# 2x2 average pooling on one core: blocks of a tile dealt out over sixteen, and engine bodies of two tiles with three result buffers

## The chip, the core and the metric

One core of a Trainium2 chip runs the kernel. Four of its instruction streams matter here: SyncE (SP), which issues the loads; VectorE (DVE), which adds; ScalarE (ACT), which scales and issues the stores; and the core's sixteen DMA engines, which move the bytes of both. The metric is the device time of one execution in microseconds (us). Before the change it is 3104.1 us, the median of nine runs that lie between 3103.82 and 3105.5.

## The reference

The input x is float32 of shape 32 x 128 x 256 x 256, kernel size and stride are 2. Each output value is the mean of a 2 x 2 window:

```python
for i in range(h_out):
    for j in range(w_out):
        window = x[:, :, i*2:i*2+2, j*2:j*2+2]
        output[:, :, i, j] = np.mean(window, axis=(2, 3))
```

The output is float32 of shape 32 x 128 x 128 x 128. So 1073.74 MB are read once and 268.44 MB are written once.

## The kernel before

The kernel views x as 524,288 rows of 512 floats: a row is the two input lines that make one output line of 128 floats. A tile is 128 partitions of 32 such rows (`TILE = 32`), that is 64 KB for each partition, 8.39 MB in all; its result is 16 KB for each partition, 2.10 MB. There are 128 tiles. `whole` is 127 of them; the last one is cut into parts of 16, 8, 4 and 4 rows a partition (`parts`), so that the end of the kernel is short.

In DRAM a tile is 128 blocks of 64 KB, one after another, and block p goes to partition p. The view `xt` says so: "(t p g) f -> t p g f". The view `ot` does the same for the result, and `block` for the parts of the last tile.

Everything stands in a critical section in which the engines' order is written out by hand, with semaphores. `take(engine, sem, n)` (line 68) waits for n and takes n off again.

- SP issues `tile_load(t, b)` (line 82, the DMA on L83) into one of two input buffers. Tiles 0 and 1 are loaded at once; every later one waits for `free[b]` first. The last tile's four parts are issued on L130, the store of tile 126 on L132. Then SP waits for the last stores: `tail`, and three of the four `stored` semaphores.
- DVE runs `tile_sum` (line 85). It waits for `loaded[b]`, adds the two input lines in place (L88), waits for the result buffer's last store (`stored[o]`, not for the first four tiles) and for its own first addition (`ready`), and adds even and odd columns into the result buffer (L92). The first four tiles are written out, then a loop has four tiles in its body, then three more are written out. The last tile's parts are on L145 and L147.
- ACT runs `tile_scale` and `tile_store` (lines 94 and 99). It waits for `summed`, gives `free[b]` to SP, multiplies by 0.25 in place (L97), waits for that, and issues the store on its own queue (L101). Again four tiles are written out, four are in the loop's body, and the rest follows. The last tile's parts are on L164 and L166.

There are four result buffers (`OUTS = 4`), taken in turn. All DMA engines serve both queues, SP's and ACT's.

Of the kernel before, what the change touches and what calls it, by code (L numbers as in the profile page):

```python
# [9 lines left out]
@with_exitstack  # L10
def kernel(
    ctx: ExitStack,
    tc: tile.TileContext,
    x: bass.AP,
    kernel_size: bass.AP,
    stride: bass.AP,
    out: bass.AP,
):
    nc = tc.nc
    P = nc.NUM_PARTITIONS  # L20

    n, c, h, w = x.shape
    k = int(kernel_size)
    s = int(stride)
    h_out = (h - k) // s + 1
    w_out = (w - k) // s + 1
    R = n * c * h_out
    units = R // P if R % P == 0 else 0


    if k == 2 and s == 2 and h % 2 == 0 and w == 256 and units >= 1024:
        _pool_2x2(ctx, tc, x, out, units)
    else:
        _generic_pool(ctx, tc, x, out, k, s, n, c, h, w, h_out, w_out)


TILE = 32
OUTS = 4


def _pool_2x2(ctx, tc, x, out, units):
    nc = tc.nc
    P = nc.NUM_PARTITIONS
    f32 = mybir.dt.float32
    w = x.shape[3]
    w_out = w // 2
    sp, act, dve = nc.sync, nc.scalar, nc.vector

    xv = x.rearrange("n c (ho a) w -> (n c ho) (a w)", a=2)
    ov = out.rearrange("n c ho wo -> (n c ho) wo")  # L50

    in_pool = ctx.enter_context(tc.tile_pool(name="inp", bufs=2))
    out_pool = ctx.enter_context(tc.tile_pool(name="outp", bufs=OUTS))
    ins = [in_pool.tile([P, TILE, 2 * w], f32, name="in_tile") for _ in range(2)]
    res = [out_pool.tile([P, TILE, w_out], f32, name="res") for _ in range(OUTS)]

    loaded = [ctx.enter_context(nc.semaphore(f"loaded{b}")) for b in range(2)]
    free = [ctx.enter_context(nc.semaphore(f"free{b}")) for b in range(2)]
    summed = ctx.enter_context(nc.semaphore("summed"))
    scaled = ctx.enter_context(nc.semaphore("scaled"))  # L60
    stored = [ctx.enter_context(nc.semaphore(f"stored{b}")) for b in range(OUTS)]
    tail = ctx.enter_context(nc.semaphore("tail"))
    ready = ctx.enter_context(nc.semaphore("ready"))
    held = ctx.enter_context(nc.semaphore("held"))

    def take(engine, sem, n=1):
        engine.wait_ge(sem, n)
        engine.sem_inc(sem, -n)  # L70

    def block(r0, g):
        rows = slice(r0, r0 + g * P)
        return xv[rows].rearrange("(p g) f -> p g f", p=P), ov[rows].rearrange("(p g) f -> p g f", p=P)

    whole, rest = divmod(units - 1, TILE)
    rest += 1
    xt = xv[0:whole * TILE * P].rearrange("(t p g) f -> t p g f", p=P, g=TILE)
    ot = ov[0:whole * TILE * P].rearrange("(t p g) f -> t p g f", p=P, g=TILE)
    loops, left = divmod(whole - OUTS, OUTS)  # L80

    def tile_load(t, b):
        sp.dma_start(out=ins[b], in_=xt[t]).then_inc(loaded[b], 16)  # L83

    def tile_sum(b, o, first=False):
        it, dst = ins[b], res[o]
        take(dve, loaded[b], 16)
        dve.tensor_add(out=it[:, :, 0:w], in0=it[:, :, 0:w], in1=it[:, :, w:]).then_inc(ready)  # L88
        if not first:
            take(dve, stored[o], 16)  # L90
        take(dve, ready)
        dve.tensor_add(out=dst, in0=it[:, :, 0:w:2], in1=it[:, :, 1:w:2]).then_inc(summed)  # L92

    def tile_scale(b, o, done):
        take(act, summed)
        act.sem_inc(free[b])
        act.mul(out=res[o], in_=res[o], mul=0.25).then_inc(done)  # L97

    def tile_store(t, o):
        take(act, scaled)  # L100
        act.dma_start(out=ot[t], in_=res[o]).then_inc(stored[o], 16)  # L101

    parts, a = [], 0
    while a < rest:
        b = rest if rest - a <= 4 else a + (rest - a) // 2
        parts.append((a, b))
        a = b

    psem = [ctx.enter_context(nc.semaphore(f"part{k}")) for k in range(len(parts))]

    with tc.tile_critical():

        for b in range(2):
            tile_load(b, b)
        with sp.Fori(2, 2 + 2 * ((whole - 2) // 2), 2) as i:
            for b in range(2):
                take(sp, free[b])
                tile_load(i + b, b)
        t = 2 + 2 * ((whole - 2) // 2)
        while t < whole:  # L120
            take(sp, free[t % 2])
            tile_load(t, t % 2)
            t += 1

        take(sp, free[whole % 2])
        it, dst = ins[whole % 2], res[whole % OUTS]
        for (a, b), s in zip(parts, psem):
            sp.dma_start(out=it[:, a:b], in_=block((whole * TILE + a) * P, b - a)[0]).then_inc(s, 16)  # L130
        take(sp, held)
        sp.dma_start(out=ot[whole - 1], in_=res[(whole - 1) % OUTS]).then_inc(stored[(whole - 1) % OUTS], 16)  # L132


        for o in range(OUTS):
            tile_sum(o % 2, o, first=True)
        with dve.Fori(0, loops) as i:
            for o in range(OUTS):
                tile_sum(o % 2, o)
        for o in range(left):  # L140
            tile_sum(o % 2, o)
        take(dve, stored[whole % OUTS], 16)
        for (a, b), s in zip(parts, psem):
            take(dve, s, 16)
            dve.tensor_add(out=it[:, a:b, 0:w], in0=it[:, a:b, 0:w], in1=it[:, a:b, w:]).then_inc(ready)  # L145
            take(dve, ready)
            dve.tensor_add(out=dst[:, a:b], in0=it[:, a:b, 0:w:2], in1=it[:, a:b, 1:w:2]).then_inc(summed)  # L147


        for t in range(OUTS):  # L150
            tile_scale(t % 2, t, scaled)
            tile_store(t, t)
        with act.Fori(OUTS, OUTS + loops * OUTS, OUTS) as i:
            for o in range(OUTS):
                tile_scale(o % 2, o, scaled)
                tile_store(i + o, o)
        for t in range(OUTS + loops * OUTS, whole):
            tile_scale(t % 2, t % OUTS, scaled if t < whole - 1 else held)
            if t < whole - 1:
                tile_store(t, t % OUTS)  # L160
        act.sem_inc(free[(whole + 1) % 2], -1)
        for a, b in parts:
            take(act, summed)
            act.mul(out=dst[:, a:b], in_=dst[:, a:b], mul=0.25).then_inc(scaled)  # L164
            take(act, scaled)
            act.dma_start(out=block((whole * TILE + a) * P, b - a)[1], in_=dst[:, a:b]).then_inc(tail, 16)  # L166


        take(sp, tail, 16 * len(parts))
        for o in range(OUTS):  # L170
            if o != whole % OUTS:
                take(sp, stored[o], 16)


def _generic_pool(ctx, tc, x, out, k, s, n, c, h, w, h_out, w_out):
# [92 lines left out]
```

## Time and profile before

| what | value |
|---|---|
| median of nine runs | 3104.1 us |
| the profiled execution's own time | 3104.78 us |
| its span in the profile | 3103.0 us |
| L88, first addition, 128x8192 | 127 times 8692 ns |
| L92, second addition, 128x4096 | 127 times 4425 ns |
| L97, scaling, 128x4096 | 127 times 3616 ns |
| load of a tile, median from issue to landing | 34.6 us |
| store of a tile, median from issue to landing | 33.9 us |
| DMA packets | 37730, 1342.21 MB |

The span is what the profiler saw between the first and the last event; the execution's own time has some more around it. In the profile, a line such as "8.69 DVE L88" in the timeline has the start, the duration, the engine and the source line of an instruction, and in brackets how long the engine was idle before it and what released it. "DVEq" is VectorE's own instruction stream, in which the waits of L70 (in `take`) stand. "SPq ... DMA_DIRECT2D" is the issue of a DMA. The DMA row of the 40 slices gives the busy share of the sixteen DMA engines in tenths. A packet is one contiguous run that one DMA engine moves: 64 KB for a load of a whole tile, 16 KB for a store of one, and 4 bytes for the write to a semaphore that each engine makes when its share has been moved.

### The profile page before, as it was taken

The page shows a single profiled execution, that of the slowest core. Times are in us where ns is not written, and L with a number is a line of the kernel's source. Part 1 is how long each engine was busy: PE and PEld are TensorE (multiplying, and loading weights), DVE is VectorE, ACT ScalarE, POOL GpSimd, SP SyncE. Part 2 cuts the span into 40 slices and gives each one's busy share as a digit, 9 for nine tenths or more (in the row PEclk, how much of TensorE's full clock was granted, in tenths as well). Part 3 has the DMA queues.
Part 4 walks back from the last instruction along what each step waited for, and adds up shares of the span by engine and source line. Part 5 has one row for each costly group of instructions (what it writes and reads, how often), then busy time and mean ns, then how long its engine had stood idle before and what let it go on. Part 6 is the DMA issues. An engine that isn't in the chain of part 4 may idle for free. (4 is left out here: it accounts for less than half of the span.)

```text
span 3103.0 us, 2444 instructions
## 1 busy us (share of the span) xinstructions
DVE 1679.7 (54%) x262; ACT 464.8 (15%) x132; POOL 0.2 (0%) x4
## 2 busy tenths in 40 slices
DVE  4555555555555555555555555555555555555555
ACT  1111111111111111111111111111111111111111
POOL 0000000000000000000000000000000000000000
DMA  9999999999999999999999999999999999999999
GB/s 415 436 439 426 436 439 425 436 440 425 437 439 425 437 439 425 437 430 434 438 439 424 441 436 424 438 439 426 436 439 424 438 440 423 438 439 423 438 438 401
DMA packets 37730, 1342.21 MB, mean 433 GB/s; under 512 B 4192, under 2 KB 4192, under 8 KB 4576
## 3 DMA queue, kind: packets, MB, share of 16 engines
q1 hardware_dynamic: 19008, 1075.85, 80.1%
q10 hardware_dynamic: 18720, 266.35, 20.1%
q14 instruction: 2, 0.02, 0.0%
HBM read 1073.74 MB, written 268.44 MB: 433 GB/s over the span
## 5 line engine op out<-in xcount | busy, mean ns | idle before, releaser
L88 DVE TENSOR_TENSOR in_tile<-in_tile 128x8192 f32<-128x8192 f32 x127 | 1103.9, 8692 | 1395.9 <-DVEq L70 1395.9
L97 ACT ACTIVATE res<-res 128x4096 f32<-128x4096 f32 x127 | 459.2, 3616 | 2587.1 <-ACTq L70 2587.1
L92 DVE TENSOR_TENSOR res<-in_tile 128x4096 f32<-128x4096 f32 x127 | 562.0, 4425 | 18.6
L145 DVE TENSOR_TENSOR in_tile<-in_tile 128x1024 f32<-128x1024 f32 (+2 forms) x4 | 9.1, 2286 | 1.3 <-DVEq L70 1.3
L97 ACT ACT_TABLE_LOAD x1 | 1.3, 1283 | 36.5 <-ACTq L70 36.5
L164 ACT ACTIVATE res<-res 128x512 f32<-128x512 f32 (+2 forms) x4 | 4.2, 1057 | 8.4 <-ACTq L70 8.4
L147 DVE TENSOR_TENSOR res<-in_tile 128x512 f32<-128x512 f32 (+2 forms) x4 | 4.9, 1225 | 0.6
L249 POOL MEMSET const-bfloat16-1.0<- 128x1 bf16 x1 | 0.1, 102 | 0.0
L249 POOL MEMSET const-uint8-127<- 128x1 uint8 x1 | 0.1, 102 | 0.0
L249 POOL MEMSET const-float32-0.0<- 128x1 f32 x1 | 0.1, 99 | 0.2 <-issue 0.2
L249 POOL MEMSET const-float32-1.0<- 128x1 f32 x1 | 0.1, 99 | 0.0
## 6 DMA issues: line engine op xcount, KB each, us to landing
out_dram<-res ACTq DMA_DIRECT2D x126, 2048.0 KB, 33.9
in_tile<-in_x_dram SPq DMA_DIRECT2D x1, 4096.0 KB, 25.1
in_tile<-in_x_dram SPq DMA_DIRECT2D x1, 2048.0 KB, 30.2
in_tile<-in_x_dram SPq DMA_DIRECT2D x2, 1024.0 KB, 33.2
out_dram<-res SPq DMA_DIRECT2D x1, 2048.0 KB, 13.8
in_tile<-in_x_dram SPq DMA_DIRECT2D x127, 34.6
out_dram<-res ACTq DMA_DIRECT2D x1, 1024.0 KB, 7.6
out_dram<-res ACTq DMA_DIRECT2D x1, 512.0 KB, 5.5
```

The lines of the kernel that those rows point to most:

```text
L88: dve.tensor_add(out=it[:, :, 0:w], in0=it[:, :, 0:w], in1=it[:, :, w:]).then_inc(ready)
L92: dve.tensor_add(out=dst, in0=it[:, :, 0:w:2], in1=it[:, :, 1:w:2]).then_inc(summed)
L97: act.mul(out=res[o], in_=res[o], mul=0.25).then_inc(done)
L145: dve.tensor_add(out=it[:, a:b, 0:w], in0=it[:, a:b, 0:w], in1=it[:, a:b, w:]).then_inc(ready)
L147: dve.tensor_add(out=dst[:, a:b], in0=it[:, a:b, 0:w:2], in1=it[:, a:b, 1:w:2]).then_inc(summed)
L164: act.mul(out=dst[:, a:b], in_=dst[:, a:b], mul=0.25).then_inc(scaled)
L249: nc = _bacc.Bacc("TRN2", target_bir_lowering=False, num_devices=1)
```

## The change

Two things are done at once.

The order by hand is written anew. There are two result buffers, taken in turn as the input buffers are, and a third one for the last tile. VectorE's loop has two tiles in its body and covers the first tiles as well; to this end each `stored[b]` is raised by 16 once before it. The wait for the result buffer's store stands ahead of the first addition now, together with the wait for the load. ScalarE's loop has two tiles in its body, with one tile written out ahead of it. The stores of tiles 125 and 126 and of the last tile's parts all raise one semaphore, `tail`, and SP waits for that alone.

The blocks of a tile are dealt out. Partition 8e + j held block 8e + j of its tile; now it holds block 16j + e, for e from 0 to 15 and j from 0 to 7. The DRAM side of each DMA has the shape 16 x 8 x run, with e outermost; the side on the chip stays 128 partitions, in their order, with one run each (`chip`). The results go back to where they belong by the same view, so the output is the same. The operations on VectorE and ScalarE keep their shapes.

```diff
-xt = xv[0:whole * TILE * P].rearrange("(t p g) f -> t p g f", p=P, g=TILE)
-ot = ov[0:whole * TILE * P].rearrange("(t p g) f -> t p g f", p=P, g=TILE)
+split = "(t j e g) f -> t e j (g f)"
+xt = xv[0:whole * TILE * P].rearrange(split, j=8, e=16, g=TILE)
+ot = ov[0:whole * TILE * P].rearrange(split, j=8, e=16, g=TILE)
...
+    def chip(tile):
+        return tile.rearrange("p g f -> p (g f)")
...
     def block(r0, g):
         rows = slice(r0, r0 + g * P)
-        return xv[rows].rearrange("(p g) f -> p g f", p=P), ov[rows].rearrange("(p g) f -> p g f", p=P)
+        split = "(j e g) f -> e j (g f)"
+        return xv[rows].rearrange(split, e=16, g=g), ov[rows].rearrange(split, e=16, g=g)
...
-    def tile_load(t, b):
-        sp.dma_start(out=ins[b], in_=xt[t]).then_inc(loaded[b], 16)
+    def load(t, b):
+        sp.dma_start(out=chip(ins[b]), in_=xt[t]).then_inc(loaded[b], 16)
...
-    out_pool = ctx.enter_context(tc.tile_pool(name="outp", bufs=OUTS))
+    out_pool = ctx.enter_context(tc.tile_pool(name="outp", bufs=3))
...
+    def sums(it, dst):
+        dve.tensor_add(out=it[:, :, 0:w], in0=it[:, :, 0:w], in1=it[:, :, w:]).then_inc(halfway)
+        take(dve, halfway)
+        dve.tensor_add(out=dst, in0=it[:, :, 0:w:2], in1=it[:, :, 1:w:2]).then_inc(summed)
+
+    def tile_sums(b):
+        take(dve, stored[b], 16)
+        take(dve, loaded[b], 16)
+        sums(ins[b], res[b])
+
+    def scale(dst, done=scaled):
+        act.mul(out=dst, in_=dst, mul=0.25).then_inc(done)
+
+    def scale_store(t, b, landed):
+        take(act, summed)
+        act.sem_inc(free[b])
+        scale(res[b])
+        take(act, scaled)
+        act.dma_start(out=ot[t], in_=chip(res[b])).then_inc(landed, 16)
...
+        for b in range(2):
+            dve.sem_inc(stored[b], 16)
+        with dve.Fori(0, whole // 2):
+            for b in range(2):
+                tile_sums(b)
+        if whole % 2:
+            tile_sums(0)
+        for a, b, part in parts:
+            take(dve, part, 16)
+            sums(it[:, a:b], dst[:, a:b])
...
+        scale_store(0, 0, stored[0])
+        pairs = (whole - 3) // 2
+        with act.Fori(1, 1 + 2 * pairs, 2) as i:
+            for b in (1, 0):
+                scale_store(i + 1 - b, b, stored[b])
+        for t in range(1 + 2 * pairs, whole - 1):
+            scale_store(t, t % 2, stored[t % 2] if t < whole - 2 else tail)
...
-        take(sp, tail, 16 * len(parts))
-        for o in range(OUTS):
-            if o != whole % OUTS:
-                take(sp, stored[o], 16)
+        take(sp, tail, 16 * (len(parts) + 2))
```

In the changed kernel the two additions stand on lines 94 and 96, the scaling on 104, the loads on 91 and 131, the stores on 111, 133 and 161.

More of the change, by code (lines that the diff above doesn't have):

```diff
@@ L37 @@
 TILE = 32
-OUTS = 4
 def _pool_2x2(ctx, tc, x, out, units):
@@ L52, in _pool_2x2, with sem @@
     in_pool = ctx.enter_context(tc.tile_pool(name="inp", bufs=2))
-    out_pool = ctx.enter_context(tc.tile_pool(name="outp", bufs=OUTS))
+    out_pool = ctx.enter_context(tc.tile_pool(name="outp", bufs=3))
     ins = [in_pool.tile([P, TILE, 2 * w], f32, name="in_tile") for _ in range(2)]
[L55 to L64, printed above, removed]
+    res = [out_pool.tile([P, TILE, w_out], f32, name="res") for _ in range(3)]
+    def sem(name):
+        return ctx.enter_context(nc.semaphore(name))
+    loaded, free, stored = [[sem(f"{n}{b}") for b in range(2)] for n in ("loaded", "free", "stored")]
+    halfway, summed, scaled, held, tail = [sem(n) for n in ("halfway", "summed", "scaled", "held", "tail")]
     def take(engine, sem, n=1):
@@ L73, in block @@
         rows = slice(r0, r0 + g * P)
-        return xv[rows].rearrange("(p g) f -> p g f", p=P), ov[rows].rearrange("(p g) f -> p g f", p=P)
+        split = "(j e g) f -> e j (g f)"
+        return xv[rows].rearrange(split, e=16, g=g), ov[rows].rearrange(split, e=16, g=g)
+    def chip(tile):
+        return tile.rearrange("p g f -> p (g f)")
     whole, rest = divmod(units - 1, TILE)
     rest += 1
-    xt = xv[0:whole * TILE * P].rearrange("(t p g) f -> t p g f", p=P, g=TILE)
-    ot = ov[0:whole * TILE * P].rearrange("(t p g) f -> t p g f", p=P, g=TILE)
-    loops, left = divmod(whole - OUTS, OUTS)
-    def tile_load(t, b):
[L83 to L101, printed above, removed]
+    split = "(t j e g) f -> t e j (g f)"
+    xt = xv[0:whole * TILE * P].rearrange(split, j=8, e=16, g=TILE)
+    ot = ov[0:whole * TILE * P].rearrange(split, j=8, e=16, g=TILE)
     parts, a = [], 0
@@ L105, in _pool_2x2 @@
         b = rest if rest - a <= 4 else a + (rest - a) // 2
-        parts.append((a, b))
+        parts.append((a, b, sem(f"part{len(parts)}")))
         a = b
-    psem = [ctx.enter_context(nc.semaphore(f"part{k}")) for k in range(len(parts))]
+    def load(t, b):
[4 more added lines that the diff above has]
+        dve.tensor_add(out=dst, in0=it[:, :, 0:w:2], in1=it[:, :, 1:w:2]).then_inc(summed)
@@ L111, in _pool_2x2 @@
+    def tile_sums(b):
[10 more added lines that the diff above has]
+        act.dma_start(out=ot[t], in_=chip(res[b])).then_inc(landed, 16)
     with tc.tile_critical():
-        for b in range(2):
-            tile_load(b, b)
@@ L115, in _pool_2x2 @@
-        with sp.Fori(2, 2 + 2 * ((whole - 2) // 2), 2) as i:
+        load(0, 0)
+        load(1, 1)
+        pairs = (whole - 2) // 2
+        with sp.Fori(2, 2 + 2 * pairs, 2) as i:
             for b in range(2):
                 take(sp, free[b])
-                tile_load(i + b, b)
-        t = 2 + 2 * ((whole - 2) // 2)
-        while t < whole:
+                load(i + b, b)
+        for t in range(2 + 2 * pairs, whole):
             take(sp, free[t % 2])
-            tile_load(t, t % 2)
-            t += 1
+            load(t, t % 2)
@@ L127, in _pool_2x2 @@
         take(sp, free[whole % 2])
-        it, dst = ins[whole % 2], res[whole % OUTS]
-        for (a, b), s in zip(parts, psem):
-            sp.dma_start(out=it[:, a:b], in_=block((whole * TILE + a) * P, b - a)[0]).then_inc(s, 16)
+        it, dst = ins[whole % 2], res[2]
+        for a, b, part in parts:
+            sp.dma_start(out=chip(it[:, a:b]), in_=block((whole * TILE + a) * P, b - a)[0]).then_inc(part, 16)
         take(sp, held)
-        sp.dma_start(out=ot[whole - 1], in_=res[(whole - 1) % OUTS]).then_inc(stored[(whole - 1) % OUTS], 16)
@@ L135, in _pool_2x2 @@
-        for o in range(OUTS):
[L136 to L147, printed above, removed]
@@ L150, in _pool_2x2 @@
[L150 to L161, printed above, removed]
@@ L162, in _pool_2x2 @@
-        for a, b in parts:
+        sp.dma_start(out=ot[whole - 1], in_=chip(res[(whole - 1) % 2])).then_inc(tail, 16)
+        for b in range(2):
[5 more added lines that the diff above has]
+            tile_sums(0)
+        for a, b, part in parts:
+            take(dve, part, 16)
+            sums(it[:, a:b], dst[:, a:b])
+        scale_store(0, 0, stored[0])
+        pairs = (whole - 3) // 2
@@ L163, in _pool_2x2 @@
+        with act.Fori(1, 1 + 2 * pairs, 2) as i:
[3 more added lines that the diff above has]
+            scale_store(t, t % 2, stored[t % 2] if t < whole - 2 else tail)
+        take(act, summed)
+        scale(res[(whole - 1) % 2], held)
+        for a, b, _ in parts:
             take(act, summed)
-            act.mul(out=dst[:, a:b], in_=dst[:, a:b], mul=0.25).then_inc(scaled)
+            scale(dst[:, a:b])
@@ L165, in _pool_2x2 @@
             take(act, scaled)
-            act.dma_start(out=block((whole * TILE + a) * P, b - a)[1], in_=dst[:, a:b]).then_inc(tail, 16)
-        take(sp, tail, 16 * len(parts))
-        for o in range(OUTS):
-            if o != whole % OUTS:
-                take(sp, stored[o], 16)
+            act.dma_start(out=block((whole * TILE + a) * P, b - a)[1], in_=chip(dst[:, a:b])).then_inc(tail, 16)
+        take(sp, tail, 16 * (len(parts) + 2))
 def _generic_pool(ctx, tc, x, out, k, s, n, c, h, w, h_out, w_out):
```

## The prediction

> **What bounds the kernel now.** I read the busy totals, then the 40 slices and the DMA queues, then the timeline of the middle and of both ends, and last the trace's records of single DMA packets.
>
> ```profile
> span 3103.0 us, 2444 instructions
> DVE 1679.7 (54%) x262; ACT 464.8 (15%) x132; POOL 0.2 (0%) x4
> ...
> DMA  9999999999999999999999999999999999999999
> ...
> q1 hardware_dynamic: 19008, 1075.85, 80.1%
> q10 hardware_dynamic: 18720, 266.35, 20.1%
> ...
> HBM read 1073.74 MB, written 268.44 MB: 433 GB/s over the span
> ```
>
> No compute engine is near full. The two queues (q1 SP: the loads, q10 ACT: the stores) together fill 100.2% of sixteen engines' span: the sixteen DMA engines are the bound, from end to end.
>
> ```profile
> 1495.34 8.69 DVE L88 TENSOR_TENSOR in_tile<-in_tile 128x8192 f32<-128x8192 f32 x1 [10.92 <-DVEq L70]
> 1504.17 4.43 DVE L92 TENSOR_TENSOR res<-in_tile 128x4096 f32<-128x4096 f32 x1
> 1508.80 3.62 ACT L97 ACTIVATE res<-res 128x4096 f32<-128x4096 f32 x1 [20.57 <-ACTq L70]
> 1508.95 48.70 SPq L83 DMA_DIRECT2D in_tile<-in_x_dram  x3
> 1512.65 0.34 ACTq L101 DMA_DIRECT2D out_dram<-res  x1
> 1519.51 8.69 DVE L88 TENSOR_TENSOR in_tile<-in_tile 128x8192 f32<-128x8192 f32 x1 [10.91 <-DVEq L70]
> ```
>
> Here one sees a tile's period: 1519.51 - 1495.34 = 24.17 us (24.19 between 3042.93 and 3067.10 at the end). VectorE stands idle 10.9 us of it and ScalarE 20.6. A load is issued at 1508.95, 13.6 us after the sums began, with the next tile's load still under way for 10.6 us. So SP has about 9 us in hand before the engines could run dry (1.3 us goes from an issue to the first packet: issued 0.96, first packet at 2.2).
>
> The packet records carry the point. An engine moves eight 64 KB packets of a load and eight 16 KB packets of a store per tile. A 64 KB packet lasts 2.418 us in the median, at the 1st percentile, and 2.420 at the 99th; a 16 KB packet 0.611 at all three. 8 x (2.418 + 0.611) = 24.2 us: the period, with nothing left. The slope, 49152 bytes in 1.807 us, is 27.2 GB/s an engine, 435 for sixteen. And the engines keep step: from the third load on, first and last of the sixteen complete 2.255 or 2.256 us apart, every time.
>
> ```profile
> 3093.98 1.22 DVE L145 TENSOR_TENSOR in_tile<-in_tile 128x1024 f32<-128x1024 f32 x1
> ...
> 3096.89 0.34 ACTq L166 DMA_DIRECT2D out_dram<-res  x1
> ```
>
> The ends are short: nothing moves for the first 2.2 us, and 9.0 us lie between the last load part's first sum and the end, of which the last store needs most. All that order, waits and buffers could give back is below 2.2 + 9.0 minus the stores that still run there: 3103.0 - 128 x 24.19 = 6.7 us, 0.2%.
>
> [...]
>
> **The change, part by part.**
>
> *Dealt-out blocks (`block`, `xt`, `ot`, `chip`).* Bytes, packets and packet sizes stay: the contiguous run is still one block of 64 KB or 16 KB. The DRAM side is now [16, 8, run] against 128 partitions. [...]
> [...] A tile's load is eight such rounds: 38.7 us. [...] Period 38.7 against 24.19: +14.5 us x 128 = +1856 us. Bounds of this unknown: nothing, [...] to 48.5 - 24.2 = 24.3 us a tile[...] (8 x 2 x 3.029 = 48.5). I take 38.7 because engines that start within 0.75 us of one another and then keep step for 127 tiles have no visible reason to drift apart by half a load[...].
> [...]
>
> *Two result buffers in place of four.* `tile_sums` now waits for the store of two tiles back before the first addition. A store is issued 17.3 us after its tile's sums began (1512.65 - 1495.34) and lands 33.9 us after that (the page's median): 51.2, and the sums of the tile two on begin at 48.4. VectorE would wait some 2.8 us, and behind it the two sums, the scaling and SP's next load, all 2.8 us later. SP has 9 us in hand: cost nothing at the period of before, and when the period grows, SP's margin grows as fast. If a store came 9 us later than that, its lateness would count in full; a store needs as many rounds as a load, so I see no cause. The third buffer frees the last tile of its wait on a store: nothing waits there in the profile (1.3 us before L145, to a load).
>
> *Loops of two tiles, fewer unrolled instructions, one last semaphore.* VectorE keeps three waits a tile, ScalarE two. A loop's end now comes every second tile, its register step and branch under VectorE's 10.9 us and ScalarE's 20.6 of idle time. The two increments that make up for the unrolled first tiles run under the 23.1 us before the first load lands. SP's four last waits become one: at the end, uncovered, a few tenths of a microsecond saved; bounds -0.5 to 0. Fewer instructions to fetch: between -1 and +1 us at the start. The diff's other edits rename.
>
> *Sum.* First packet 2.2, 128 loads at 38.7 = 4954, from the last landing to the end 9.0: 4965 us span. The runs' median stands 1.1 us over the profiled span (its own execution took 3104.78): 4966, and I write 4965.
>
> **The rivals.**
>
> *In step to the last (slower, more).* If partners are less than a store packet apart, [...]: round 4.836 + 0.611, period 43.6, 5590 us; with reads sharing as well 48.5 and 6215. For: the constant 2.255 us and starts within 0.75 us. Against: the order of packets differs between engines once stores begin.
>
> *Staggered pairs (slower, less).* If one partner is favoured a little each time they meet, its lead grows [...]. Its lead is limited: its next load is issued 13.6 us after the slower partner's landing and starts 1.3 later, so the lead is at most P - 15 where half of P is wanted. With conflict rounds for the rest, P = 24.2 + 4.836 x (4 - 8(P - 15)/P), which gives 26.7 us: 3425 us. Halfway there, with a lead that grows over the run, 3500 to 4600. For: only a lasting bias of a per cent or two in sharing is needed. Against: nothing in the trace drifts.
>
> *[...] (the other side: not slower).* [...] Then the period stays 24.2 us, the other edits are worth -1.5 to +1, and the time is 3102 to 3105. [...] A new bound on VectorE is out: 13.3 us of work in 24.2.
>
> **How the numbers follow.** Forecast (36 to 41 us a tile, 4620 to 5260): 0.36. In step: 0.18. Staggered, from 3170 to 4620: 0.33. [...] 0.13, of which 0.10 is within 0.2% (6 us, about what a measurement of this kernel can tell from no change), 0.02 faster by more, 0.01 slower. So slower 0.88. [...]
>
> **What would show it.** In the profile after: fewer GB/s at an unchanged number of packets and bytes, in every slice; the queues' packet time still near the whole span, since packets last longer (64 KB toward 4.8 us, not 2.4); VectorE's durations (8.69, 4.43) unchanged with longer idle time before L94, put down to a load. Wrong, if the 64 KB packets still last 2.418 us and the period is 24.2; or if the packets keep 2.4 us and engines stand idle, when the wait for stores or SP's issue would be the cause. A period that falls along the run speaks for the stagger.

## The result and the profile after

The changed kernel takes 5443.42 us, the median of ten runs between 5374.82 and 5496.24, against 3103.95 for the kernel before. The ratio of the two is 1.748, with a 95% interval from 1.745 to 1.751. Here and below a ratio leaves out runs over 1.5% longer than the shortest of the same kernel (two here, four of `deal_stores`). The profiled execution took 5418.58 us, its span is 5416.8.

From the page of the changed kernel, the span and the busy totals, the DMA and rate rows of the 40 slices, the DMA queues and the packets:

```profile
span 5416.8 us, 2614 instructions
...
DVE 1679.6 (31%) x262; ACT 464.7 (9%) x132; POOL 0.2 (0%) x4
...
DMA  9999999999999999999999999999999999999999
GB/s 226 244 246 243 243 245 247 244 246 246 243 246 245 246 245 246 245 249 247 251 252 250 252 255 254 250 253 253 253 250 251 252 254 251 253 252 252 247 247 235
DMA packets 37728, 1342.19 MB, mean 248 GB/s; under 512 B 4192, under 2 KB 4192, under 8 KB 4576
...
q1 hardware_dynamic: 19008, 1075.85, 85.2%
q10 hardware_dynamic: 18720, 266.35, 14.8%
```

Bytes and packet sizes are those of before, and VectorE and ScalarE are busy for the same microseconds. The DMA engines are still "busy" from end to end, but move 248 GB/s, not 433. A busy share of nines says nothing of speed here: a packet that lasts longer counts as busy for longer. The rate row of the kernel before has no slice under 401:

```profile
GB/s 415 436 439 426 436 439 425 436 440 425 437 439 425 437 439 425 437 430 434 438 439 424 441 436 424 438 439 426 436 439 424 438 440 423 438 439 423 438 438 401
```

So the loss is in every slice, and it is neither start nor end.

A tile in the middle, from the timeline (start, duration, engine, line, operation, idle time before):

```profile
2697.23 8.69 DVE L94 TENSOR_TENSOR in_tile<-in_tile 128x8192 f32<-128x8192 f32 x1 [28.67 <-DVEq L67]
2706.07 4.42 DVE L96 TENSOR_TENSOR res<-in_tile 128x4096 f32<-128x4096 f32 x1
2710.70 3.62 ACT L104 ACTIVATE res<-res 128x4096 f32<-128x4096 f32 x1 [38.31 <-ACTq L67]
2710.85 42.36 SPq L91 DMA_DIRECT2D in_tile<-in_x_dram  x2
2714.57 0.55 ACTq L111 DMA_DIRECT2D out_dram<-res  x1
2739.04 8.69 DVE L94 TENSOR_TENSOR in_tile<-in_tile 128x8192 f32<-128x8192 f32 x1 [28.55 <-DVEq L67]
```

The period is 41.8 us here, where it was 24.2. The sums last as long as ever; VectorE's idle time grew from 10.9 to 28.6 us. In the trace's packet records a 64 KB load packet lasts 4.50 us in the mean (2.42 before) and a 16 KB store packet 0.786 (0.611 before): 8 x (4.50 + 0.786) = 42.3 us, which is again the whole period: the sums of tiles 0 to 126 start 42.3 us apart in the mean.

### The profile page after: what moved, and what is told of

Its sections match the earlier page's. It is cut to its first block, busy times and chain, and to the rows that moved or that the text cites. A ratio compares the mean times of both kernels' runs of the same rounds, so it can differ in the third digit from the quotient of the medians.

```text
span 5416.8 us, 2614 instructions
## 1 busy us (share of the span) xinstructions
DVE 1679.6 (31%) x262; ACT 464.7 (9%) x132; POOL 0.2 (0%) x4
## 5 line engine op out<-in xcount | busy, mean ns | idle before, releaser
L94 DVE TENSOR_TENSOR in_tile<-in_tile 128x8192 f32<-128x8192 f32 (+1 forms) x131 | 1113.0, 8496 | 3708.2 <-DVEq L67 3708.2
L104 ACT ACTIVATE res<-res 128x4096 f32<-128x4096 f32 (+1 forms) x131 | 463.5, 3538 | 4884.8 <-ACTq L67 4884.8
L96 DVE TENSOR_TENSOR res<-in_tile 128x4096 f32<-128x4096 f32 (+1 forms) x131 | 566.9, 4327 | 19.2
```

What stands on the lines that cost most here:

```text
L104: act.mul(out=dst, in_=dst, mul=0.25).then_inc(done)
```

## The experiments

Three questions: which half of the change costs, whether it is the place in DRAM or the shape of the transfer against the chip's 128 partitions, and what in it makes a packet slow.

The prediction's 38.7 us a tile is 8 x 4.836, with 4.836 = 2 x 2.418: it supposes that the engines stand in pairs, and that two partners need twice 2.418 us to move a 64 KB packet each. That is its author's estimate, worked out from the 2.418 us of before. No trace of before shows such a pair.

### The order alone, the dealing alone

`order_only` is the changed kernel with the plain views; `deal_only` is the kernel before with the dealt views (and `chip`).

```diff
 order_only, against the changed kernel
-    split = "(t j e g) f -> t e j (g f)"
+    split = "(t p g) f -> t p (g f)"
...
-        split = "(j e g) f -> e j (g f)"
+        split = "(p g) f -> p (g f)"
```

> The changed order, two result buffers and one last semaphore, with block p of a tile on partition p as before. Theory [...]: 3102 to 3105 us, a period of 24.2 us, 64 KB packets of 2.42 us. Rival (the two result buffers or the earlier wait for the store hold up the loads): well over 3110 us, up to the changed kernel's 5443, with idle time of VectorE put down to stores.

> The kernel before, with its four result buffers and its order, and only the views dealt out (16 x 8 on the DRAM side). [...] 5350 to 5500 us, as the changed kernel. Rival of the buffers: about 3104 us.

`order_only` took 3103.67 us, ratio 0.9999 (0.999 to 1.0007): nothing gained, nothing lost. `deal_only` took 5355.5 and 5438.0 us in its two timed runs, close to the changed kernel. So the dealing is the whole of the change's cost, whichever order stands around it. A tile of `order_only`:

```profile
1496.97 8.69 DVE L94 TENSOR_TENSOR in_tile<-in_tile 128x8192 f32<-128x8192 f32 x1 [10.93 <-DVEq L67]
...
1521.18 8.69 DVE L94 TENSOR_TENSOR in_tile<-in_tile 128x8192 f32<-128x8192 f32 x1 [10.94 <-DVEq L67]
```

The period is 24.2 us as before. The wait for a store, now ahead of the first addition, can be seen in the trace: from the third tile on the sums start about 3.3 us after their load has landed, and right after a store has; before the change it was 0.14 us after the load. SP's loads go out 3 us later for that and land when they did (31.5 us after their issue in the median, 34.6 before). The 9 us in hand swallow it.

### DRAM or partitions

`own_sixteenth` keeps the 16 x 8 shape, but moves the blocks of the sixteen outer indices 66.6 MB apart in DRAM. `own_128th` has a DRAM side that isn't contiguous either, but its outer dimension is 128. (Its parts of the last tile are plain too, which the cut below leaves out.)

```diff
 own_sixteenth
-    split = "(t j e g) f -> t e j (g f)"
+    split = "(e t j g) f -> t e j (g f)"
 own_128th
-    split = "(t j e g) f -> t e j (g f)"
+    split = "(p t g) f -> t p (g f)"
```

> The changed kernel with another dealing of the first 127 tiles: DRAM side still 16 x 8 x run, but each outer index has its own sixteenth of the input and walks through it block by block, so that the sixteen engines read 65 MB apart and not in one stretch of 1 MB. [...] 5200 to 5650 us, 64 KB packets near 4.5 us. Rival (sixteen engines in one stretch of DRAM hinder each other there): about 3104 us.

> The changed order with each partition walking through its own 128th of the input: the DRAM side is 128 x run with a step of 8 MB between partitions, not contiguous. [...] about 3104 us, 64 KB packets of 2.42 us. Rival (any DRAM side that isn't one contiguous stretch costs this much): about 5440 us. A DRAM pitch that itself hurts would show as packets longer than 2.42 us and a time in between.

`own_sixteenth`: 5469 us, ratio 1.762 (1.759 to 1.765). `own_128th`: 3103.61 us, ratio 0.9999 (0.999 to 1.0008), 64 KB packets of 2.418 us from the 1st to the 90th percentile. The queues of the two (packets, MB, share of sixteen engines' span) show it; first `own_sixteenth`:

```profile
q1 hardware_dynamic: 19008, 1075.85, 85.3%
q10 hardware_dynamic: 18720, 266.35, 14.7%
```

and `own_128th`:

```profile
q1 hardware_dynamic: 19008, 1075.85, 80.1%
q10 hardware_dynamic: 18720, 266.35, 20.1%
```

The loads' share rises from 80 to 85% because their packets got longer by more than the stores' did (from the shares and the spans of 3103.0 and 5461.6 us: 1.87 times against 1.29). Where the blocks lie in DRAM makes half a per cent at most here (5469 us against 5443). What the slow ones have in common is the outer dimension of 16 against 128 partitions.

### Loads or stores

In `deal_loads` and `deal_stores` one of the two views is plain. `loads_only` leaves the stores of tiles 0 to 125 out.

```diff
 deal_stores
-    xt = xv[0:whole * TILE * P].rearrange(split, j=8, e=16, g=TILE)
+    xt = xv[0:whole * TILE * P].rearrange("(t p g) f -> t p (g f)", p=P, g=TILE)
 loads_only
-        act.dma_start(out=ot[t], in_=chip(res[b])).then_inc(landed, 16)
+        act.sem_inc(landed, 16)
```

> The changed kernel with the stores' blocks in their plain places and only the loads dealt out (the output's rows are permuted within a tile). [...] the loads carry it, 5250 to 5500 us. Rival (dealt stores carry a good part): under 5000.

> The changed kernel with the loads' blocks in their plain places and only the stores dealt out (the output's rows are permuted within a tile). [...] If reads share as writes do: 16 KB packets up to 1.22 us, a period up to 24.2 + 4.9 = 29.1 us and a time up to 3730. If reads do not: about 3104 us, 16 KB packets of 0.61 us.

> The changed kernel without the stores of the first 126 tiles (that part of the output is left unwritten); loads, sums and scaling as they are. [...] every 64 KB packet lasts 2 x 2.418 = 4.836 us, the period is 38.7 us and the time 4950 to 4970; the 42.4 of the changed kernel is then 38.7 plus a part of the stores' 4.9 that the partner does not hide. If engines in one pair drift apart by themselves, less: 3000 to 4700. [...]

`deal_loads` took 5383 us (1.734, 1.720 to 1.749). `deal_stores` took 3118 us in the median, ratio 1.0038 (1.0021 to 1.0054), with 16 KB packets at 0.611 us up to the 90th percentile. Its eighteen runs spread from 3107 to 3164 us, where the kernel before stays within 1.3 us beside them: dealt stores cost 0.1 to 1.9%, differently from run to run. The dealt loads cost the rest: it is the transfers that write into the chip's partitions that suffer. (Whether two readers would hinder each other as much when they meet, this run does not tell: the stores take a fifth of the engines' time, 20.1% before the change, and may seldom fall together. Some store packets did last up to 1.53 us.)

`loads_only` took 5185 us (1.671, 1.660 to 1.681), more than the 4950 to 4970 expected. Two tiles of its timeline:

```profile
528.23 8.69 DVE L94 TENSOR_TENSOR in_tile<-in_tile 128x8192 f32<-128x8192 f32 x1 [27.04 <-DVEq L67]
...
568.52 8.69 DVE L94 TENSOR_TENSOR in_tile<-in_tile 128x8192 f32<-128x8192 f32 x1 [27.03 <-DVEq L67]
```

The period is 40.3 us without a store in it. Its packets come in fours, all engines alike: one of about 4.88 us, then three of 5.10. What sets the fours the trace doesn't show. For a pair as the prediction supposes it, two packets of 64 KB in 5.10 us make an estimate of 25.7 GB/s (26.0 with the mean packet of 5.04), less than the 27.2 that each engine moved before. The stores of the changed kernel then cost 42.3 - 40.3 = 2.0 us a tile: their packets take 8 x 0.786 = 6.3 us, and the load packets get 8 x (5.04 - 4.50) = 4.3 us shorter beside them.

### Is it sharing, or an engine by itself?

An engine could also be slow by itself in a dealt load, whatever the others do. `four_engines` has the first four outer indices alone, `eight_engines` the first eight. Both leave the rest of the output unwritten.

```diff
+ENGINES = 4
...
-        return tile.rearrange("p g f -> p (g f)")
+        return tile[0:8 * ENGINES].rearrange("p g f -> p (g f)")
...
-        sp.dma_start(out=chip(ins[b]), in_=xt[t]).then_inc(loaded[b], 16)
+        sp.dma_start(out=chip(ins[b]), in_=xt[t][0:ENGINES]).then_inc(loaded[b], 16)
```

> The changed kernel on the first 32 partitions alone (a quarter of each tile's blocks; the rest of the output is left unwritten): outer size 4, so that four engines work[...]. Theory [...]: 64 KB packets of 2.42 us, a time near 3100. Rival [...]: packets of 4.5 to 5.1 us, 5000 to 5450.

> The same on the first 64 partitions, outer size 8 (half of the output is left unwritten): [...] Theory: packets near 4.5 us and 5250 to 5500 us, with half of the bytes of the changed kernel. Rival (the sixteen together are too much for something all use): clearly shorter packets, down to 2.42 us and 3100.

`four_engines`: 3102.33 us (ratio 0.9994, 0.9984 to 1.0004), packets of 2.418 us. Its queues:

```profile
q1 hardware_dynamic: 4752, 268.96, 20.0%
q10 hardware_dynamic: 4680, 66.59, 5.0%
```

These are a quarter of the shares of before, in the time of before: four of sixteen engines are at work, with packets as short as in the plain transfer. `eight_engines`: 4922.8 and 5094.3 us, with half the bytes of the changed kernel and packets of 4.20 us in the mean. That is below both expected figures (5250 us, 4.5 us); why eight engines lose a little less than sixteen stays open. So the slowness comes with the other engines: the first four outer indices alone have packets of 2.418 us, and with the next four beside them the mean is 4.20.

### Can the partners be kept apart?

`nudge` lays small extra loads ahead of the first loads (21 times, the last at 923 us), meant to put one packet more on one engine of each supposed pair. `eight_apart` takes the eight outer indices and lays four loads of four 64 KB packets each ahead of everything, into partitions 64 to 79: meant as four packets, 4 x 2.418 = 9.7 us, on each of the first four engines. `eight_apart_loads` is the same without stores.

```diff
 nudge
+    def nudge():
+        sp.dma_start(out=chip(spare[0:12]), in_=xt[0][0:12, 0, 0:TILE * w_out]).then_inc(nudged, 16)
+        sp.dma_start(out=chip(spare[32:36]), in_=xt[0][0:4, 0, 0:TILE * w_out]).then_inc(nudged, 16)
 eight_apart
+        for k in range(4):
+            sp.dma_start(out=ins[0][64 + k:80 + k:4].rearrange("p g f -> p (g f)"), in_=xt[k][0:4, 0]).then_inc(nudged, 16)
         load(0, 0)
```

> The changed kernel with more work: ahead of each of the first 22 loads, two small extra loads into a spare tile, of 12 and of 4 partitions with 16 KB each[...]. Theory [...]: the period falls from about 43 us to 25 to 30 in the first fifth of the run and stays there, 3400 to 4000 us. Rivals (what costs is the place in DRAM[...]): 5440 plus the extra packets, 5440 to 5480 us.

> As on 64 partitions, but four packets of 64 KB ahead of the first load, for engines 0 to 3 alone and into partitions that nothing else uses[...]: 9.7 us, half a load[...]. If the phase decides and stays: 64 KB packets of 2.4 to 3.2 us, a period of 25 to 30 us, 3300 to 3900 us. If pairs are drawn back into step: short packets in the first tiles, then 4.5 us again, 4800 to 5450. If the phase does not matter: 4.5 us from the first tile on, about 5450.

> The same without the stores of the first 126 tiles: [...] If the phase decides and stays: a period of 22 to 26 us, 2850 to 3350 us. If pairs are drawn back without stores too: packets from 2.4 rising to 5.1 us, 4500 to 5185. If the phase does not matter: 5.1 us at once, about 5190.

`nudge` did not do what it was meant to: 5471 us (1.763, 1.743 to 1.782), no better than without. Its rate row:

```profile
GB/s 221 235 246 251 236 238 243 254 255 265 260 262 258 255 248 251 247 246 241 245 243 245 242 244 241 246 240 246 241 245 242 245 241 240 246 240 245 242 244 235
```

The rate climbs to 265 in the tenth slice, some 300 us after the last extra load, and then falls back to 240. The experiment was badly sized: an extra packet lasted 0.97 us in the median and up to 2.56, and not 0.61. How far the pairs were pushed is not known, so the run doesn't tell whether phase matters, that is, how far one engine is in its load when another writes. `eight_apart` does. Its stages (from:to, length, DVE busy, ACT, POOL, clock, DMA share, GB/s):

```profile
0.00:150.00 150.00, 54.47 (x9) 15.75 (x5) 0.20 (x4) 1.00 0.49 178
150.00:300.00 150.00, 70.53 (x11) 18.08 (x5) 0.00 (x0) 1.00 0.50 186
300.00:450.00 150.00, 58.41 (x10) 18.08 (x5) 0.00 (x0) 1.00 0.50 154
450.00:600.00 150.00, 52.40 (x8) 14.46 (x4) 0.00 (x0) 1.00 0.50 146
...
900.00:1500.00 600.00, 198.65 (x31) 57.86 (x16) 0.00 (x0) 1.00 0.50 134
1500.00:3000.00 1500.00, 484.70 (x74) 133.79 (x37) 0.00 (x0) 1.00 0.50 130
3000.00:4900.00 1900.00, 615.70 (x94) 169.96 (x47) 0.00 (x0) 1.00 0.50 129
```

`eight_engines` is the same kernel without the four packets ahead. Its rate row, in slices of 127 us:

```profile
GB/s 117 135 131 127 129 131 128 127 130 132 135 135 134 131 132 131 130 132 132 133 132 134 135 135 133 132 133 132 133 132 134 133 132 138 144 139 127 129 127 126
```

Half of sixteen engines at full speed would be 217 GB/s. Set apart, the eight do 186 between 150 and 300 us, where they do 131 to 135 without; then they fall to 129, the rate of `eight_engines`. Over the whole run the gain is lost: 4958 us (1.597, 1.590 to 1.604), between the two runs of `eight_engines`. The timeline at the start and the same kernel without stores:

```profile
147.93 8.68 DVE L96 TENSOR_TENSOR in_tile<-in_tile 64x8192 f32<-64x8192 f32 x1 [15.05 <-DVEq L68]
...
176.22 8.68 DVE L96 TENSOR_TENSOR in_tile<-in_tile 64x8192 f32<-64x8192 f32 x1 [15.04 <-DVEq L68]
```

```profile
994.65 8.68 DVE L96 TENSOR_TENSOR in_tile<-in_tile 64x8192 f32<-64x8192 f32 x1 [11.19 <-DVEq L68]
...
1019.10 8.68 DVE L96 TENSOR_TENSOR in_tile<-in_tile 64x8192 f32<-64x8192 f32 x1 [11.20 <-DVEq L68]
```

28.3 us a tile while apart, with stores; 24.4 us without them, and there it stays so to the end: `eight_apart_loads` took 3159.7 us, where all sixteen took 5185 in `loads_only`. Eight engines here and sixteen there, but an engine has the same packets in both, and one delay of 9.7 us at the start stands against some 2000 us; eight engines without stores and without that delay were not run. Even apart, the loads alone need more than the 8 x 2.418 = 19.3 us that they last unhindered: a tenth of their packets last over 3.6 us. So what costs is which writes fall together in time, and a delay of some of them at the start takes most of it away (24.4 us a tile against 40.3, loads alone); at what they meet no run shows. With stores among the loads the gain is gone within some 1500 us; why stays open.

No run of the whole work beat the kernel before by more than its measurement can tell. `order_only` equals it with shorter loop bodies and three result buffers.

## Why the prediction was right, and where it was not

- *The bound and the direction.* Right. The DMA engines were full, a 64 KB packet lasted 2.418 us, the shortest seen in any run, and nothing was won by reading neighbouring blocks: `own_sixteenth` and `own_128th` show no effect of the place in DRAM above half a per cent.
- *The mechanism.* Right in what costs: engines that get in each other's way when they write at one time. `four_engines` against `eight_engines` (packets of 2.418 and 4.20 us), and `eight_apart` against `eight_engines` in the first 300 us (186 GB/s and 131 to 135), leave no other cause that was proposed. That they do so two by two, and which two, is the author's supposition and was not shown: the packet records don't name partitions. Pairs that move what one engine moved before, 27.2 GB/s, make an estimate of 8 x 27.2 = 218 GB/s, and `loads_only` moved 209.
- *The size.* 4965 was too low by 478 us, and the time lies above the forecast's own 4620 to 5260, inside the wider range of 3300 to 5700: what was held likeliest did not come true. Two terms were sized too low. The 4.836 us of a load packet: `loads_only` has 5.04 in the mean, 40.3 us a tile instead of 38.7; 5185 - 4965 = 220 us. The stores, for which the 38.7 us have no time at all: they cost 2.0 us a tile; 5443 - 5185 = 258 us. The two make up the 478. Two small readings are off as well: at the end the period is 3067.10 - 3042.93 = 24.17 us and not 24.19, and the first packet starts at 2.0 us and not 2.2. With 24.17 the bound on order, waits and buffers is 9.2 us and not 6.7; nothing hangs on it.
- *The in-step rival.* Its 43.6 us and 5590 came nearest. The loads in the trace land 43.3 to 43.6 us apart in tiles 2 to 6, and mostly 41 to 43 later. But it had the parts wrong: load packets of 4.836 and stores of 0.611 one after the other. The first eighth of the run has 4.63 and 0.79: beside stores a load packet is shorter than the 5.04 of `loads_only`, and a store packet is longer than 0.611.
- *The staggered rival.* For engines that are set apart its formula comes near: it gave 26.7 us, and `eight_apart` began at 28.3. For loads alone, with 8 x 2.418 = 19.3 in place of its 24.2, it gives 24.1, and 24.4 was measured. But with stores the gain doesn't last, and in the changed kernel it hardly comes about.
- *"Nothing in the trace drifts."* Wrong for the changed kernel: first and last of the sixteen completions of a load lie 1.2 us apart in the first tile and up to 28.9 near the end, about the lead of P - 15 = 27.3 us that the rival allowed. The period fell along the run, the sign named for it, but only from 43.6 to about 41.7 us. So engines do drift apart, at little gain. Whether partners or whole pairs do so stays open: the records don't say which engine is whose partner.
- *Result buffers, waits, loops, one semaphore.* Right: costed at nothing, with 2.8 us of waiting (3.1 measured) hidden under SP's 9. `order_only` differs from before by 0.3 us in the median, inside its interval.

## What to carry to other kernels

In a load from DRAM into 128 partitions, look at the outermost dimension of the DRAM side: at 128 a 64 KB packet lasted 2.418 us here, at 16 it lasted 5.04 us in the loads alone, which took 2.1 times as long (40.3 us a tile against 8 x 2.418), with the same bytes and packet sizes. Where the place in DRAM must be rearranged, keep 128 outermost; `own_128th` did so at no cost (3103.61 us, ratio 0.9999). And divide the bytes of a packet by its time: a full DMA row in the profile went with 248 GB/s here as well as with 433.

## What was not expected of the hardware

- Load packets that fall together took more than twice their time: 5.10 us in `loads_only`, three of every four, against 2.418 in the plain transfer and the 4.836 of the estimate.
- Dealing out the stores costs 0.4% (ratio 1.0038), dealing out the loads 73%: with the stores alone dealt, store packets stayed at 0.611 us up to the 90th percentile.
- Engines meant to be set apart by 9.7 us stay fast without stores over 128 tiles (24.4 us a tile throughout). With stores they lose the gain: 28.3 us a tile at the start, about 40 from tile 31 on.
